# A six-deep weight ring for the last two jobs of the attention output projection, and one set of row buffers for w_o

## The chip, the core and the metric

The kernel runs on one core of a Trainium2 chip. The engines named below are TensorE (PE, with its weight loads shown as PEld), VectorE (DVE), ScalarE (ACT), GpSimd (POOL) and SyncE (SP, which issues most DMA transfers; ACT issues some). Each engine carries out its own instructions in the order in which they stand, and waits on semaphores for the others. The metric is the device time of one execution in microseconds (us), the median of several runs.

## The reference

One layer of a decoder block on a sequence of 2048 positions with 1024 channels:

```python
proj = h @ w_in[l]
...
y_rnn = (hr * jax.nn.silu(z_rnn.astype(jnp.float32))).astype(dt) @ w_out_rnn[l]
...
o = dilated_attention_mixture(qh, kh, vh).reshape(B, S, D_ATTN)
y_attn = (o * jax.nn.silu(z_attn.astype(jnp.float32))).astype(dt) @ w_out_attn[l]
...
merged = jax.nn.sigmoid(g_r + bg_r) * y_rnn + jax.nn.sigmoid(g_a + bg_a) * y_attn
x = x + gate[:, None, :] * (merged @ w_o[l])
return rms_norm(x, g_final)
```

The part that matters here is the product with `w_out_attn` (the second half of its columns), the merging behind it, and the product with `w_o`.

## The kernel before

Every fp32 product is made of three matmuls (`mm3`): each factor is split into a high part, rounded by ACT (`hi_act`), and a low part, the difference, made by DVE or POOL (`lo_dve`, `lo_pool`); high x high, high x low and low x high are added in PSUM.

The projections with `w_out_rnn` and `w_out_attn` are the generator `steps(jobs)`. A job is one of the two weight matrices with 512 positions; there are eight, the last four for attention. A job has 8 output tiles of 128 x 512, a tile 8 steps (one block of 128 input channels each), a step 3 matmuls. The weights of a tile come in two halves of 4 steps. Halves are numbered through all jobs by `x`; the last two jobs are tiles 48 to 63 (`TAIL0` is 48), steps 0 to 127 and halves 96 to 127. The first six jobs are worked off in between the attention heads; the last two run alone, one after the other, with the preparation of the output projection beside them.

Halves up to `RAW` = 97 come already split from DRAM (`wD`, 512 KB each). Later ones come raw (`wR`, 256 KB) and are split in place: `load_w(x)` loads into the second plane of the tile, `split_w(x)` writes the high part into the first plane and the low part over the raw values. The tiles of the ring are S0 to S3. `load_w(x + 3)` stands behind the first step of half x, `split_w(x + 1)` ahead of it; the low part is POOL's for every fourth half and DVE's else. The buffer that `load_w` writes was last read by half x - 1, so SP waits for PE there.

In the same steps: `load_g` loads two tiles (gaT and mrT, into the ring fg or into s1 and s2) for the eviction of a tile, `evict` multiplies the PSUM tile with one and adds the other (two DVE instructions), `store` writes the sum to meT; `load_y` and `split_y` load and split the 8 tiles of attention output for the next job (yh, yl; POOL for even, DVE for odd ones), around the boundary between the two jobs at step 64.

The output projection uses one level of Strassen's scheme. Its right factors (B11, B21, B22, T1 to T4, each high and low) are made of w_o in four builds, k = 0 to 3. A build takes two rows of w_o of 128 x 1024 (`load_rows(k)`, 512 KB each), multiplies each with the gate on POOL (`gate_rows`), combines their quarters on DVE (`combine`), and splits seven results (`high` on ACT; the low parts of B22, T3 and T1 on POOL, the others on DVE). The last two are those of T4 and T1. The rows stand in st1 and st2 for even k, in st3 and st4 for odd k; st0 holds the gate. `build_rows(s, k)` puts the pieces behind steps s to s + 16 of the last two jobs, with s = 10, 34, 74 and 98; the rows are loaded ahead of step 0 and behind steps 16, 44 and 75, by SP for k = 0 and by ACT else.

Behind the builds come the left factors of the first pair of rows of the output: `load_left(0)` loads two blocks of meT into st1 and st2 behind step 104, `left_events` sums and splits them into st3, st4, st0 and S0 to S3. Then the product phase begins: eight calls of `output_pair`, each with seven products of 12 matmuls into X, Z, W, V, X, Y and V. At its start a pool is opened, x rows and g_final are loaded by SP (`load_rows_x`), and then the A tiles of the second pair by `load_left(1)`, which is fired by `fire_p`.

All this stands under a manual schedule: the engines' queues are in the order in which the code calls the instructions. In each step of the last two jobs the generator's own instructions come first, then what `on(n, ...)` put behind that step.

Of the kernel before, what the change touches and what calls it, by code (L numbers as in the profile page):

```python
# [10 lines left out]
F32 = mybir.dt.float32  # L11
# [9 lines left out]
P = 128  # L21
S = 2048
# [67 lines left out]
def decoder_block(ctx, tc, x, c, positions, g_norm, w_mod, b_mod, w_in, b_gate, conv_w, conv_b,  # L90
# [1567 lines left out]
    def steps(jobs):  # L1658

        tiles = [(j, m) for j in range(len(jobs)) for m in range(KT)]  # L1660
        Y, G = {}, {}

        def load_w(x):

            if x < 2 * len(tiles):
                assert x == n_w[0]
                j, m = tiles[x // 2]
                if x <= RAW:
                    load_wd(jobs[j][0], m, x % 2)
                    return  # L1670

                n_w[0] += 1
                W[x] = t = T(pS, [P, 2, KH, P], F32R, f"S{x % 4}")
                nc.sync.dma_start(t[:, 1].bitcast(F32), wR[m, x % 2])

        def split_w(x):
            if RAW < x < 2 * len(tiles):
                raw = W[x][:, 1].bitcast(F32)
                hi_act(W[x][:, 0], raw)
                (lo_pool if x % 4 == 0 else lo_dve)(W[x][:, 1], raw, W[x][:, 0])  # L1680

        def load_y(j, k):
            if j < len(jobs):
                w, ys, n = jobs[j]
                if ys is oT and (n, k) == (2, KT - 1):

                    Y0[False, n, k] = last_head[0].zt[:, 0].rearrange("p r j -> p (r j)")
                    return
                if ys is oT and n == 2 and k >= KH:

                    t = T(ap_, [P, KQW], F32, "kraw", bufs=4)
                    nc.sync.dma_start(t[:, :CH], ys[k * P : (k + 1) * P, n * CH : (n + 1) * CH])
                    Y0[False, n, k] = t[:, :CH]
                    return
                assert ys is yaT or (n // 2, k, n % 2) in stored
                load_yd(ys, n, k)

        def split_y(j, k):
            if j < len(jobs):
                Y[j, k] = yh, yl = [T(fl, [P, CH], F32R, tag, bufs=NY) for tag in ("yh", "yl")]  # L1700
                w, ys, n = jobs[j]
                t = Y0.pop((ys is yaT, n, k))
                hi_act(yh[:], t[:])
                (lo_dve if k % 2 else lo_pool)(yl[:], t[:], yh[:])

        def load_g(t):
            j, m = tiles[t]
            w, ys, n = jobs[j]
            at_ = slice(m * P, (m + 1) * P), slice(n * CH, (n + 1) * CH)
            G[t] = []  # L1710
            for src in (grT,) if ys is yaT else (gaT, mrT):
                if t >= TAIL0 and (t - TAIL0) % 3 == 2 and t < TAIL0 + 13:
                    g = T(fp, [P, CH], F32, ("s1", "s2")[len(G[t])])
                else:
                    g = T(fl, [P, CH], F32, "fg", bufs=4)
                nc.sync.dma_start(g[:], src[at_])
                G[t].append(g)

        def evict(t, ps):
            g = G[t]  # L1720
            nc.vector.tensor_tensor(g[0][:], ps[:], g[0][:], ALU.mult)
            if len(g) > 1:
                nc.vector.tensor_tensor(g[0][:], g[0][:], g[1][:], ALU.add)

        def store(t):
            j, m = tiles[t]
            w, ys, n = jobs[j]
            nc.sync.dma_start((mrT if ys is yaT else meT)[m * P : (m + 1) * P, n * CH : (n + 1) * CH], G.pop(t)[0][:])

        g_loads = {(0, 0): [0], (14, 0): [14], (15, 0): [15]}  # L1730
        for x in range(13):
            g_loads[x, 3] = [x + 1]
        for k in range(KT):
            split_y(0, k)
        yield
        last = None
        for t, (j, m) in enumerate(tiles):
            ps = T(pj, [P, CH], F32, "pj")
            for k in range(KT):
                if k % KH == 0:  # L1740
                    split_w(2 * t + k // KH + 1)
                if k % KH == 1:

                    load_w(2 * t + k // KH + 3)
                if k == 1 and t:
                    evict(t - 1, last)
                if t < TAIL0:
                    if k == 3:
                        load_g(t)
                    if k == 7 and t:  # L1750
                        store(t - 1)
                else:
                    if k == 4:
                        store(t - 1)
                    for x in g_loads.pop((t - TAIL0, k), ()):
                        load_g(TAIL0 + x)
                wt = W[2 * t + k // KH]
                yh, yl = Y[j, k]
                mm3(ps[:], wt[:, 0, k % KH, :], wt[:, 1, k % KH, :], yh[:], yl[:], first=k == 0, last=k == KT - 1)
                if k % KH == KH - 1:  # L1760
                    W.pop(2 * t + k // KH)


                x = m * KT + k - KT * (KT - 1)
                j1 = j + 1
                if m == 0:
                    x, j1 = x + KT * KT, j

                if j1 == NB + 2:

                    if -14 <= x < KT - 14:
                        load_y(j1, x + 14)
                elif j1 and x in LOAD_Y:
                    load_y(j1, LOAD_Y[x])
                if j1 and x in SPLIT_Y:
                    split_y(j1, SPLIT_Y[x])
                yield
            last = ps
        evict(len(tiles) - 1, last)
        store(len(tiles) - 1)  # L1780
# [72 lines left out]
    v = {}  # L1853
    tt = nc.vector.tensor_tensor

    def load_rows(k):
        for i in range(2):
            v[k, i] = t = stage(1 + i + 2 * (k % 2), [P, D])
            (nc.scalar if k else nc.sync).dma_start(t[:], w_o[0, (k + i * KH) * P : (k + i * KH + 1) * P, :])

    def gate_rows(k, i):
        nc.gpsimd.tensor_tensor(v[k, i][:], v[k, i][:], v["gate"][:], ALU.mult)
# [26 lines left out]
    A, ops = {}, {}  # L1889
    NP = 2 * NB  # L1890

    def load_left(p):
        for half in range(2):
            shape = [P, KH, 2 * P]
            A[p, half] = t = T(up[0], shape, F32, f"A{half}", bufs=2) if p else stage(1 + half, shape)
            (nc.sync if p else nc.scalar).dma_start(t[:], meT[half * KH * P : (half + 1) * KH * P, p * 2 * P : (p + 1) * 2 * P]
# [164 lines left out]
    with tc.manual_schedule():  # L2061
        v["gate"] = stage(0, [P, D])
        nc.sync.dma_start(v["gate"][:], gateD[0:1, :].broadcast_to([P, D]))
        load_rows(0)
        for k in range(KH):
            build_rows((10, 34, 74, 98)[k], k)
            if k:
                on((16, 44, 75)[k - 1], load_rows, k)
        on(LAST - 24, load_left, 0)
        early = {}  # L2070
        for p in range(NP):
            for d, fn, args in left_events(p):
                x = 7 * p + d - 4
                if p or d > 2:
                    on_p(max(x, 1), fn, *args)
                else:
                    on(LAST - 12 + 4 * (d + 1), fn, *args)
            if p:
                on_p(max(7 * p - 12, 0), load_left, p)
            if p > 1:  # L2080
# [6 lines left out]
        assert not pend  # L2087
        pools.close("fl", "pR")
        up.append(pools.open("up", side="right", bufs=1))
        v["gf"] = T(up[0], [P, D], F32, "gf")  # L2090
        load_rows_x(0)
        load_rows_x(1)
        nc.sync.dma_start(v["gf"][:], g_final.unsqueeze(0).broadcast_to([P, D]))
        fire_p()
        for p in range(NP):
            output_pair(p)
        assert not after
# [30 lines left out]
```

## Time and profile before

| what | value |
| --- | --- |
| median of 3 runs | 2246.54 us (2245.64 to 2247.35) |
| the profiled execution | 2248.86 us |
| its span, first to last instruction | 2247.1 us, 34124 instructions |
| mean granted TensorE clock | 0.990 |
| the last two jobs, half 96 to the first product of the output projection | 1963.11 to 2083.84 us of the span |
| product phase | 2083.84 to the end |

In the views, a time is in us from the span's start. A row of the timeline has start, duration, engine, line, operation, output <- inputs, and in brackets the idle time ahead of it and what ended it. A row of the view of waits has who waited for whom, total us, number, longest. A row of the groups has busy us, mean ns of one, then idle us ahead of them with what ended it. L150 is the matmul in `mm`, L158 `hi_act`, L164 `lo_pool`, L167 `lo_dve`; L1674 is `load_w`, L1716 `load_g`, L1721 and L1723 the eviction, L1862 `gate_rows`. SPq and ACTq are issues of transfers. A row of the DMA view has the number of issues, KB each and median us from issue to landing.

### The profile page before, as it was taken

How to read it: one execution, taken by the hardware profiler on the slowest of the kernel's cores; microseconds unless marked ns; L12 is line 12 of the kernel's file. 1: busy time of each engine (PE TensorE's matmuls, PEld its weight loads, DVE VectorE, ACT ScalarE, POOL GpSimd, SP SyncE). 2: the span in 40 equal slices, each digit the busy share in tenths (PEclk: the TensorE clock that was granted, in tenths of full speed). 3: DMA queues.
4: the chain of work that ended last, by engine and by line, in shares of the span. 5: the costliest groups of instructions: out<-in, count | busy, mean ns of one | idle time of the engine just before them, and what ended most of it. 6: DMA issues, size and time to landing. Idle time of an engine off the chain costs nothing. (4 is left out here: it accounts for less than half of the span.)

```text
span 2247.1 us, 34124 instructions
## 1 busy us (share of the span) xinstructions
PE 2179.4 (97%) x11326; PEld 1837.1 (82%) x11326; DVE 1437.4 (64%) x2475; ACT 1283.2 (57%) x2554; POOL 1072.3 (48%) x791
## 2 busy tenths in 40 slices
PE   8999999999999999999999999999999998978998
PEld 5998888888778988888788877888888887856786
DVE  5839887878455715445445352566667787678787
ACT  6638678767533627556547202676778877533333
POOL 2457677667556322222223112555556555445443
PEclk9999999999999999999999999999999999999999
DMA  8367887887998378898889989988988887877543
GB/s 285 117 213 261 280 302 265 299 279 259 327 285 281 107 234 277 274 298 287 284 299 300 355 294 293 282 270 248 275 257 262 248 255 220 262 253 237 178 163 113
DMA packets 412133, 577.34 MB, mean 257 GB/s; under 512 B 72406, under 2 KB 270258, under 8 KB 410932
## 3 DMA queue, kind: packets, MB, share of 16 engines
q1 hardware_dynamic: 369748, 446.75, 63.5%
q10 hardware_dynamic: 42016, 128.36, 14.9%
q8 instruction: 90, 1.47, 0.3%
q14 instruction: 87, 0.71, 0.1%
q0 software_dynamic: 192, 0.05, 0.0%
HBM read 356.92 MB, written 218.11 MB: 256 GB/s over the span
## 5 line engine op out<-in xcount | busy, mean ns | idle before, releaser
L150 PE MATMUL pj<-yh,S 128*128 128x512 f32 x1024 | 372.9, 410 | 24.0 <-ACT S L158 7.0
L164 POOL TENSOR_TENSOR S<-R,S 128x512 fp32r<-128x512 f32 x168 | 256.1, 1533 | 172.8 <-ACT S L158 66.7
L150 PE MATMUL X<-T,S 128*128 128x512 f32 x1344 | 327.4, 393 | 7.0 <-ACT u L384 3.6
L150 PE MATMUL V<-T,S 128*128 128x512 f32 x1344 | 324.4, 390 | 0.5 <-DVE t L454 0.3
L150 PEld LDWEIGHTS X<-T,S 128*128 128x128 f32 x1344 | 253.1, 189 | 62.8 <-ACT u L384 5.1
L150 PEld LDWEIGHTS V<-T,S 128*128 128x128 f32 x1344 | 252.0, 188 | 54.5 <-DVE t L454 0.7
L150 PEld LDWEIGHTS pj<-yh,S 128*128 128x128 f32 x1024 | 194.7, 191 | 68.5 <-ACT S L158 9.0
L150 PE MATMUL pj<-yl,S 128*128 128x512 f32 x512 | 205.1, 401 | 8.7 <-POOL yl L164 5.6
L164 POOL TENSOR_TENSOR S<-s,S 128x512 fp32r<-128x512 f32 x92 | 139.7, 1518 | 112.4 <-ACT S L158 72.0
L1421 ACT ACTIVATE pp<-pp,st 128x256 f32<-128x256 f32 (+3 forms) x256 | 133.8, 524 | 93.4 <-DVE st L1420 92.2
L150 PE MATMUL Y<-T,S 128*128 128x512 f32 x672 | 163.2, 392 | 0.0
L150 PE MATMUL Z<-T,S 128*128 128x512 f32 x672 | 161.9, 390 | 0.0
L150 PE MATMUL W<-T,S 128*128 128x512 f32 x672 | 161.6, 389 | 0.0
L150 PEld LDWEIGHTS Y<-T,S 128*128 128x128 f32 x672 | 127.1, 190 | 26.5
L150 PEld LDWEIGHTS W<-T,S 128*128 128x128 f32 x672 | 126.0, 188 | 27.0 <-issue 0.9
L150 PEld LDWEIGHTS Z<-T,S 128*128 128x128 f32 x672 | 125.8, 188 | 26.0
L167 DVE TENSOR_TENSOR ptl<-pT,pth 128x384 fp32r<-128x384 f32 (+1 forms) x160 | 97.9, 629 | 75.1 <-ACT pth L158 72.8
L164 POOL TENSOR_TENSOR s<-R,s 128x512 fp32r<-128x512 f32 x32 | 45.5, 1421 | 207.3 <-ACT s L158 176.4
L912 DVE SCALAR_TENSOR_TENSOR xc<-xr,par,xc 128x512 f32<-128x512 f32 x96 | 98.4, 1025 | 48.4 <-ACT xc L906 46.2
L158 ACT ACTIVATE S<-R 128x512 fp32r<-128x512 f32 x168 | 101.6, 622 | 45.6 <-DMA R<-in_w_in_dram 20.0
L1485 ACT ACTIVATE pp<-pp,M 128x256 f32<-128x256 f32 (+3 forms) x256 | 118.0, 523 | 9.9 <-DVE M L1608 9.9
L150 PEld LDWEIGHTS pj<-yl,S 128*128 128x128 f32 x512 | 98.4, 192 | 28.2 <-POOL yl L164 8.3
(401 smaller groups left out, 4867.0 us busy)
## 6 DMA issues: line engine op xcount, KB each, us to landing
sD<-S ACTq DMA_DIRECT2D x196, 512.0 KB, 4.2
S<-sD SPq DMA_DIRECT2D x196, 512.0 KB, 5.2
S<-wD SPq DMA_DIRECT2D x98, 512.0 KB, 5.5
R<-in_w_in_dram SPq DMA_DIRECT2D x136, 256.0 KB, 4.2
wD<-s ACTq DMA_DIRECT2D x64, 256.0 KB, 5.3
T<-in_w_mod_dram SPq DMA_DIRECT2D x8, 1024.0 KB, 11.8
vN<-ev SPq DMA_DIRECT2D x64, 128.0 KB, 2.8
zaT<-ev SPq DMA_DIRECT2D x32, 256.0 KB, 4.6
```

Of the source, the lines that this page charges most:

```text
L150: nc.tensor.matmul(o, lhsT=l, rhs=r, start=st, stop=sp, **kw)
L158: nc.scalar.activation(o, i, AF.Copy)
L164: nc.gpsimd.tensor_tensor(o, i, h.bitcast(F32), ALU.subtract)
L167: return nc.vector.tensor_tensor(o, i, h.bitcast(F32), ALU.subtract).ins
L912: nc.vector.scalar_tensor_tensor(xc, xr[:, i : i + CH], cw(i), xc, ALU.mult, ALU.add)
L1421: nc.scalar.activation(pdst, pdst, AF.Exp, bias=m_, scale=-1.0, accum_out=l_)
L1485: nc.scalar.activation(pp, pp, AF.Copy, scale=w)
```

## The change

The raw halves use a ring of six tiles, S0 to S3, st3 and st4. In the last two jobs, raw loads are five halves ahead of use (behind the first step of half x, half x + 5; behind the first step of half 96, halves 99, 100 and 101) and splits three ahead (behind the second step of half x, half x + 3; 98 in half 96, 99 and 100 in half 97). The low part is POOL's for odd halves and DVE's for even ones. As st3 and st4 belong to the ring, all four builds use st1 and st2 for their rows; a row is loaded behind step s - 8 or s - 4 of its build, with s = 8, 32, 68 and 92. The two blocks of meT are loaded behind steps 107 and 110, and the first left operands' steps are 118, 121, 124 and 127 instead of 116, 120, 124 and 128. At the start of the product phase `fire_p`, and with it the load of the A tiles, stands ahead of the loads of the x rows and of g_final.

```diff
-                W[x] = t = T(pS, [P, 2, KH, P], F32R, f"S{x % 4}")
+                i = (x - 2 * TAIL0) % 6
+                W[x] = t = T(pS, [P, 2, KH, P], F32R, f"S{i}") if i < 4 else T(fp, [P, 2, KH, P], F32R, f"st{i - 1}")
                 nc.sync.dma_start(t[:, 1].bitcast(F32), wR[m, x % 2])
...
-                (lo_pool if x % 4 == 0 else lo_dve)(W[x][:, 1], raw, W[x][:, 0])
+                (lo_pool if x % 2 else lo_dve)(W[x][:, 1], raw, W[x][:, 0])
...
-                if k % KH == 0:
-                    split_w(2 * t + k // KH + 1)
+                x = 2 * t + k // KH
                 if k % KH == 1:
 
-                    load_w(2 * t + k // KH + 3)
+                    if x < 2 * TAIL0:
+                        load_w(x + 3)
+                    for x1 in range(x + 3 if x == 2 * TAIL0 else x + 5, x + 6) if x >= 2 * TAIL0 else ():
+                        load_w(x1)
+                if k % KH == 2 and x >= 2 * TAIL0:
+                    for x1 in (x + 2, x + 3) if x == 2 * TAIL0 + 1 else (x + 2,) if x == 2 * TAIL0 else (x + 3,):
+                        split_w(x1)
...
-    def load_rows(k):
-        for i in range(2):
-            v[k, i] = t = stage(1 + i + 2 * (k % 2), [P, D])
-            (nc.scalar if k else nc.sync).dma_start(t[:], w_o[0, (k + i * KH) * P : (k + i * KH + 1) * P, :])
+    def load_rows(k, i):
+        v[k, i] = t = stage(1 + i, [P, D])
+        (nc.scalar if k else nc.sync).dma_start(t[:], w_o[0, (k + i * KH) * P : (k + i * KH + 1) * P, :])
...
-    def load_left(p):
-        for half in range(2):
+    def load_left(p, halves=range(2)):
+        for half in halves:
...
-        load_rows(0)
-        for k in range(KH):
-            build_rows((10, 34, 74, 98)[k], k)
-            if k:
-                on((16, 44, 75)[k - 1], load_rows, k)
-        on(LAST - 24, load_left, 0)
-        early = {}
+        for k, x in enumerate((8, 32, 68, 92)):
+            build_rows(x, k)
+            for i in range(2):
+                on(max(x - 8 + 4 * i, 0), load_rows, k, i)
+        on(107, load_left, 0, (0,))
+        on(110, load_left, 0, (1,))
...
-                    on(LAST - 12 + 4 * (d + 1), fn, *args)
+                    on(LAST - 10 + 3 * (d + 1), fn, *args)
...
-        v["gf"] = T(up[0], [P, D], F32, "gf")
+        fire_p()
         load_rows_x(0)
         load_rows_x(1)
+        v["gf"] = T(up[0], [P, D], F32, "gf")
         nc.sync.dma_start(v["gf"][:], g_final.unsqueeze(0).broadcast_to([P, D]))
-        fire_p()
```

## The prediction

> **What bounds the kernel now.** I began with the page: TensorE is busy for 97% of the span, so the question is where it stands still or runs slowly. The view of busy time by stretches was cut at the places the change touches: the whole of the last two jobs, then that stretch cut at the starts of halves 105, 111 and 114, and the first products behind it. (A half is one half tile of weights, numbered as in the code; halves 96 to 127 belong to the last two jobs. Columns: stretch, length, busy time and count of PE, PEld, DVE, ACT, POOL, granted clock, DMA share, GB/s.) The last row, from the chain of waits, is a product at full pace.
>
> ```profile
> PE 2179.4 (97%) x11326; PEld 1837.1 (82%) x11326; DVE 1437.4 (64%) x2475; ACT 1283.2 (57%) x2554; POOL 1072.3 (48%) x791
> ...
> 1963.11:2083.84 120.73, 100.45 (x386) 73.92 (x384) 93.42 (x97) 41.67 (x72) 61.50 (x34) 0.94 0.75 240
> 1963.11:2001.78 38.67, 30.40 (x110) 21.48 (x108) 23.47 (x26) 10.02 (x17) 16.41 (x9) 0.91 0.74 252
> 2001.78:2023.36 21.58, 17.51 (x74) 13.20 (x72) 20.79 (x21) 8.41 (x14) 11.54 (x7) 1.00 0.87 260
> 2023.36:2038.73 15.37, 11.51 (x37) 6.96 (x36) 9.54 (x9) 6.23 (x11) 8.75 (x5) 0.89 0.91 282
> 2038.73:2083.84 45.11, 41.03 (x170) 32.28 (x168) 39.61 (x43) 17.02 (x31) 24.80 (x14) 0.96 0.65 207
> ...
> 2112.64 2.72 PE V L150 x12
> ```
>
> Twelve matmuls take 2.72 us, so the 32 halves need 32 x 2.72 = 87.0 us; they take 120.73. The 33.7 us over are 14.2, 5.3, 7.2 and 7.0 in the four stretches (9, 6, 3 and 14 halves). Next the waits in this window, and then the rows of PE, SP and ACT around the costliest one.
>
> ```profile
> ACT S L158 <- DMA S<-wR: 40.4, 12, 6.9
> ...
> PE pj L150 <- ACT S L158: 7.0, 4, 2.6
> PE pj L150 <- DVE S L167: 5.3, 5, 2.3
> PE pj L150 <- POOL S L164: 4.0, 4, 1.7
> ...
> 1976.19 1.06 PE L150 MATMUL pj<-yh,S 128*128 128x512 f32 x2
> ...
> 1981.62 0.64 PE L150 MATMUL pj<-yh,S 128*128 128x512 f32 x1 [2.63 <-ACT S L158]
> ...
> 1966.23 0.33 SPq L1716 DMA_DIRECT2D fg<-mrT  x1
> 1966.61 0.43 SPq L1674 DMA_DIRECT2D S<-wR  x1
> 1967.81 0.32 SPq L1716 DMA_DIRECT2D fg<-gaT  x1
> 1976.15 0.32 SPq L1716 DMA_DIRECT2D fg<-mrT  x1
> ...
> 1977.04 0.89 SPq L1674 DMA_DIRECT2D S<-wR  x2
> ...
> 1980.94 0.63 ACT L158 ACTIVATE S<-S 128x512 fp32r<-128x512 f32 x1 [6.87 <-DMA S<-wR]
> ```
>
> PE waits for weights that are split late, and they are split late because ACT waits for raw loads. These are late in their turn because SP stood from 1967.81 to 1976.15 at the mrT load: its buffer comes free with an eviction on VectorE that is queued behind the split of half 99, which waits for the load issued at 1966.61. It is a loop: one late load delays the issue of the next. After such a wait PE also runs at half pace (two matmuls in 1.06 us, where 2.72/12 = 0.23 us apart is usual), and the first stretch's granted clock is 0.91.
>
> The other limit is the pair VectorE and GpSimd, which turn the rows of w_o into Strassen factors ("builds" 0 to 3) beside the jobs:
>
> ```profile
> 1997.58 1.71 POOL L164 TENSOR_TENSOR S<-S 128x512 fp32r<-128x512 f32 x1
> 1999.25 5.65 POOL L1862 TENSOR_TENSOR st<-st,st 128x1024 f32<-128x1024 f32 x2
> ...
> 2000.47 2.18 DVE L1723 TENSOR_TENSOR fg<-fg,fg 128x512 f32<-128x512 f32 x1
> 2002.57 3.48 DVE L167 TENSOR_TENSOR S<-S 128x512 fp32r<-128x512 f32 x2
> ...
> L164 POOL TENSOR_TENSOR S<-S 128x512 fp32r<-128x512 f32 x7 | 10.3, 1477 | 24.2 <-ACT S L158 19.2 <-DMA S<-wR 5.0
> L167 DVE TENSOR_TENSOR S<-S 128x512 fp32r<-128x512 f32 x23 | 25.7, 1125 | 17.9 <-ACT S L158 17.9
> ...
> 2025.35 1.30 POOL L164 TENSOR_TENSOR S<-S 128x512 fp32r<-128x512 f32 x1 [5.00 <-DMA S<-wR]
> 2005.98 0.68 DVE L167 TENSOR_TENSOR B11l<-st,B11h 128x512 fp32r<-128x512 f32 x1
> ```
>
> While GpSimd multiplies two rows, VectorE subtractions of 0.68 us take 2.18 and 3.48 for two: they end when the GpSimd instruction ends. So the two engines share one resource for these operations.
>
> **The change, part by part.** Outside the last two jobs nothing moves. Number and size of loads, matmuls and splits stay, so there the cost is nothing; what alters is where they stand.
>
> (1) Loads five ahead. Loads 99, 100 and 101 now go out together right behind the mrT load of 1966.23, ahead of the one that stood until 1976.15, so 100 and 101 are issued some 9 us earlier. That takes away the wait of 2.63 us and the slow matmuls behind it; the wait for half 99 (its load goes out at the same place) I leave. Later loads get 4.75 instead of 2.75 halves, 12.9 instead of 7.5 us, of which landing takes 4.3 (row below). SP still waits at each for PE to leave the buffer, at the same place in its queue, and what is behind it (mrT, gaT, stores) sees nothing new.
>
> (2) Splits three ahead, every second one on GpSimd: GpSimd gets 15 of them instead of 7, VectorE 15 instead of 23. A weight now may be late by 2.5 halves, 6.8 us, before PE notices. In the changed order half 105's subtraction stands on GpSimd right behind the last one (T1l) of build 0, half 111's right behind that of build 1, 127's behind that of build 3. So there PE waits for the build.
>
> (3) One set of row buffers. A row load now waits on ACT's queue until the build before has read the buffer; the second row's until T1l is done. ACT's splits of later halves are queued behind it. Before, it was issued half a build ahead. Exposed are: build 1's row, build 3's row, and the half of meT that the first left operands need. Build 2's is not: its rows come while GpSimd does the yl of the job boundary.
>
> (4) First left operands and, behind the jobs, A ahead of xo and gf in SP's queue.
>
> ```profile
> 1982.88 2.82 POOL L1862 TENSOR_TENSOR st<-st,st 128x1024 f32<-128x1024 f32 x1
> ...
> 1995.89 1.73 POOL L164 TENSOR_TENSOR T1l<-st,T1h 128x512 fp32r<-128x512 f32 x1 [4.53 <-ACT T1h L158]
> ...
> 2016.94 1.74 POOL L164 TENSOR_TENSOR T1l<-st,T1h 128x512 fp32r<-128x512 f32 x1 [3.81 <-ACT T1h L158]
> ...
> 2040.20 2.85 POOL L1862 TENSOR_TENSOR st<-st,st 128x1024 f32<-128x1024 f32 x1
> ...
> 2053.59 1.73 POOL L164 TENSOR_TENSOR T1l<-st,T1h 128x512 fp32r<-128x512 f32 x1 [4.54 <-ACT T1h L158]
> ...
> 2025.18 1.66 ACT L158 ACTIVATE yh<-R 128x512 fp32r<-128x512 f32 x3
> ...
> S<-wR SPq DMA_DIRECT2D x29, 256.0 KB, 4.3
> st<-in_w_o_dram ACTq DMA_DIRECT2D x6, 512.0 KB, 7.5
> R<-oT SPq DMA_DIRECT2D x8, 256.0 KB, 5.1
> ...
> S<-wD SPq DMA_DIRECT2D x98, 512.0 KB, 5.5
> ...
> 2086.56 0.39 PE L150 MATMUL Z<-T2h,st 128*128 128x512 f32 x1
> ...
> 2101.09 0.73 PE L150 MATMUL X<-B11h,st 128*128 128x512 f32 x2 [0.32 <-DVE st L167]
> 2107.36 0.73 PE L150 MATMUL Z<-T2h,st 128*128 128x512 f32 x2 [0.48 <-POOL st L164]
> ```
>
> What a lone row load takes is not shown: rows were loaded in pairs, 7.5 us each. Bounds: 4.3 (256 KB) and 7.5 (the pair); I take 5.5, as other 512 KB loads, plus 0.6 for semaphore and issue. From the end of the second row's product to T1l's end build 2 took 2055.32 - 2043.05 = 12.3 us and build 1 2018.68 - 2004.90 = 13.8; I take 12.3 (12.8 for build 3), since fewer late splits sit between. The sum follows this chain:
>
> Half 105: build 0's second row goes out at about 1977, behind the same mrT wait, and lands at 1981.3 to 1984.5; before, its product ran from 1982.88 to 1985.70, held by a split ahead of it in the queue. So T1l still ends at 1997.6. The split of 105 follows (1.3 to 1.7), and the half starts two matmuls before it: 1998.7, against 2001.78: 3.1 us ahead.
>
> Half 111: 1997.6 + 6.1 (row) + 2.8 + 12.3 = 2018.8 for T1l, split 2020.3, start 2019.9 against 2023.36: 3.5 ahead.
>
> Half 114: GpSimd does yl0 (to 2021.6), the split of 113 (2022.9), yl2 (2024.2); then y6 can be loaded (5.1), split (0.6 + 1.3): 2031.2; 114 starts 1.4 later, 2032.6 against 2038.73: 6.1 ahead. This needs the yh of 2025.18 to come earlier; it stood behind splits waiting for raw loads.
>
> First Z: two row products (5.2) and 12.3: T1l of build 2 at 2048.7; row 6.1, product 2.8, build 12.8: 2070.4; half of meT 6.1; two sums on VectorE, ACT and GpSimd (2 x 0.68 + 0.63 + 1.4 = 3.4): 2079.9 against 2086.56, 6.7 ahead. PE alone would be there at 2032.6 + 38.1 + 2.7 = 2073.4, and so waits; a half-pace stretch like that of 1976 behind such a wait costs up to 1.7 us. That leaves 5.0. A ahead of xo saves 0.5 of the waits of 0.32 and 0.48; the xo loads have cover, as they are added last.
>
> Sum: 5.5 us. The profiled execution took 2248.86 (span 2247.1), so 2243.4 by its own time. The median of the runs, 2246.54, lies 2.3 lower: 2241.0.
>
> The eight subtractions moved to GpSimd hold the shared resource for 1.30 (row at 2025.35) instead of 0.68 us (row at 2005.98) each, 5.0 us more together. I count those on the chain above and hold the rest covered by the row loads' landing. [...]
>
> **Rivals.** (a) Exposed rows decide: slower. If lone row loads land in 7.5 us too and builds take 13.8: T1l of build 1 at 1997.6 + 8.1 + 2.8 + 13.8 = 2022.3, half 111 level; 114 at 2036.1; T1l of build 2 at 2054.1, of build 3 at 2078.8; meT half 8.1, 3.4: Z at 2090.3, 3.7 late, with the slow stretch 5.4: 2252. It decides from about 6.5 us a row on. For it: DMA shares of 0.74 to 0.91. Against it: single loads instead of pairs.
> (b) The shared resource decides: no cover, 5.0 us back: 2246.0. For it: VectorE and GpSimd are busy for 93.42 + 61.50 us of 120.73. Against it: waiting for each other is counted in that (a split takes 1477 and 1125 ns in the mean, 1.30 and 0.68 us alone), and GpSimd stood idle for 24.2 us ahead of its seven splits.
> (c) Rows land in 4.3 us and no half-pace stretch: three exposures of 1.2 us less and 1.7: 2241.0 - 5.3 = 2235.7. For it: GB/s of 207 in the last stretch.
>
> **How the numbers follow.** Forecast 0.44 (its own range 2237 to 2245), (a) 0.14, (b) 0.25, (c) 0.17. A measurement of this kernel tells about 0.2%, 4.5 us, from no change: faster is below 2242.0, slower above 2251.0. Forecast: 0.34 faster, 0.10 same. (b): 0.04, 0.19, 0.02 slower. (a): 0.02 same, 0.12 slower. (c): all faster. Faster 0.55, same 0.31, slower 0.14. The range runs from 2232 ((c) with half 99's wait gone too) to 2251.5, just short of (a).
>
> **What would show it.** No PE wait at the start of half 100; 40.4 us of ACT waits on wR nearly gone; PE waits at 105 and 111 for POOL; a POOL or ACT wait for a lone w_o row of about 5 us in builds 1 and 3; PE waiting for Z's operand. Wrong if T1l of build 1 ends after 2021, if SP still stands ahead of loads 100 and 101, or if PE still waits at every second half.

## The result and the profile after

| | median, us | range, us | runs | ratio to before |
| --- | --- | --- | --- | --- |
| before, on the same chip | 2246.02 | 2245.19 to 2247.74 | 8 | |
| after | 2251.72 | 2248.41 to 2255.43 | 8 | 1.0024, interval 1.0013 to 1.0035 |

The change made the kernel slower by 0.24%, 5.7 us; the prediction was 2241.0. On another chip the same kernel came out at 1.0028 (interval 1.0014 to 1.0042), so the loss is the kernel's. The profiled execution of after took 2251.41 us, its span 2249.6 (before: 2248.86 and 2247.1).

These are the stretches of after: the last two jobs, and these cut at the starts of halves 105, 111 and 114, with the columns of the prediction's first view.

```profile
1962.02:2087.85 125.83, 101.34 (x386) 77.67 (x384) 95.07 (x89) 41.22 (x71) 72.35 (x40) 0.89 0.73 230
1962.02:2001.99 39.97, 28.96 (x110) 21.69 (x108) 22.82 (x23) 11.71 (x20) 18.07 (x11) 0.91 0.70 221
2001.99:2025.51 23.52, 18.97 (x73) 14.91 (x72) 20.79 (x21) 9.96 (x17) 17.21 (x10) 0.85 0.83 256
2025.51:2041.18 15.67, 11.21 (x38) 7.62 (x36) 9.95 (x8) 4.13 (x7) 9.12 (x6) 0.81 0.88 298
2041.18:2087.85 46.67, 42.21 (x170) 33.45 (x168) 41.51 (x40) 15.42 (x27) 27.95 (x16) 0.92 0.65 201
```

The last two jobs took 125.83 us instead of 120.73. Each of the four stretches is longer, by 1.3, 1.9, 0.3 and 1.6. The product phase, from there to the end of the span, took 161.8 instead of 163.3 us, 1.5 less; part (4) of the change stands there (see before_fire below).

Next, PE's waits in the last two jobs of after (who waits for whom, total us, times, longest).

```profile
PE pj L150 <- DVE s L1722: 6.5, 2, 4.5
PE pj L150 <- DVE fg L1722: 5.9, 2, 5.4
PE pj L150 <- ACT yh L158: 5.3, 3, 2.9
PE pj L150 <- ACT T4h L158: 3.4, 1, 3.4
PE pj L150 <- POOL S L164: 1.0, 2, 0.6
PE pj L150 <- ACT S L158: 0.9, 1, 0.9
...
```

The change did what it says to the waits for weights: 7.0 + 5.3 + 4.0 = 16.3 us became 1.0 + 0.9 = 1.9. But a wait that before does not have took their place: L1722 is the eviction. The first matmul of an output tile waits until the tile two earlier has been read, since these tiles have two PSUM buffers. With the one named T4h, at whose end VectorE had just done an eviction (it ended at 2074.16, the matmul started at 2074.31), these are 6.5 + 5.9 + 3.4 = 15.8 us. The waits for the next job's left operands (yh and, in the rows left out, yl) went from 3.8 to 6.5. All waits of the view together rose from 20.1 to 24.2 us, and PE's busy time rose from 100.45 to 101.34: nearly the whole 5.1 us. So the lower granted clock (0.89 instead of 0.94) shows in at most the 0.9 us of busy time.

The rows behind the longest wait, in after: those of SP, then VectorE, and one or two each of POOL, ACT and PE.

```profile
1967.01 0.38 SPq L1675 DMA_DIRECT2D S<-wR  x1
1967.44 0.90 SPq L1675 DMA_DIRECT2D st<-wR  x2
1968.39 0.84 SPq L1717 DMA_DIRECT2D fg<-gaT  x1
1978.90 0.32 SPq L1717 DMA_DIRECT2D fg<-mrT  x1
...
1979.74 0.43 SPq L1864 DMA_DIRECT2D st<-in_w_o_dram  x1
1980.27 0.93 SPq L1675 DMA_DIRECT2D S<-wR  x2
```

```profile
1974.81 1.26 DVE L167 TENSOR_TENSOR st<-st 128x512 fp32r<-128x512 f32 x1 [5.15 <-ACT st L158]
1975.99 0.68 DVE L1722 TENSOR_TENSOR fg<-pj,fg 128x512 f32<-128x512 f32 x1
1976.70 2.17 DVE L1724 TENSOR_TENSOR fg<-fg,fg 128x512 f32<-128x512 f32 x1
1985.96 1.64 DVE L167 TENSOR_TENSOR S<-S 128x512 fp32r<-128x512 f32 x1 [7.08 <-ACT S L158]
1987.53 0.68 DVE L167 TENSOR_TENSOR B11l<-st,B11h 128x512 fp32r<-128x512 f32 x1
1988.13 0.68 DVE L1722 TENSOR_TENSOR fg<-pj,fg 128x512 f32<-128x512 f32 x1
```

```profile
1975.48 2.85 POOL L1867 TENSOR_TENSOR st<-st,st 128x1024 f32<-128x1024 f32 x1
1984.71 2.35 POOL L1867 TENSOR_TENSOR st<-st,st 128x1024 f32<-128x1024 f32 x1 [4.68 <-DMA st<-in_w_o_dram]
1985.30 0.63 ACT L158 ACTIVATE S<-S 128x512 fp32r<-128x512 f32 x1 [6.31 <-DMA S<-wR]
1988.95 0.77 PE L150 MATMUL pj<-yh,S 128*128 128x512 f32 x1 [5.38 <-DVE fg L1722]
```

Read them from the top. Halves 99, 100 and 101 are loaded together at 1967.01 to 1968.34, as the prediction had it. SP then stands at the mrT load of tile 49 until 1978.90: 10.5 us after the gaT load, where before it was 8.3. It is released 0.03 us behind the end of the eviction of tile 48 (1976.70 + 2.17). That eviction stands on VectorE behind the split of half 100 (1974.81), which had itself waited 5.15; and its addition took 2.17 us instead of 0.69 (before, at 1975.43), as GpSimd was multiplying a row (1975.48). Behind the mrT load on SP stand the second row of build 0 (1979.74; POOL waits 4.68 for it) and the raw weights of halves 102 and 103 (1980.27). Those of 102 are split at 1985.30, VectorE takes the low part at 1985.96 after 7.08 idle, and only then, behind a low part of the build, at 1988.13, it evicts the tile that PE waits for. PE was free at 1988.95 - 5.38 = 1983.57: half 102's own weights, complete at 1987.60, come 4.0 us late, and the eviction queued behind them adds the last 1.3.

The wait at half 110 has the same form, without any late load (ACT's rows of after, then VectorE's and PE's):

```profile
2016.76 0.63 ACT L158 ACTIVATE T4h<-st 128x512 fp32r<-128x512 f32 x1 [1.79 <-DVE st L1875]
2017.30 0.61 ACT L158 ACTIVATE S<-S 128x512 fp32r<-128x512 f32 x1
```

```profile
2017.94 0.69 DVE L167 TENSOR_TENSOR S<-S 128x512 fp32r<-128x512 f32 x1 [0.61 <-ACT S L158]
...
2019.15 0.69 DVE L167 TENSOR_TENSOR T4l<-st,T4h 128x512 fp32r<-128x512 f32 x1
2019.76 0.69 DVE L1722 TENSOR_TENSOR s<-pj,s 128x512 f32<-128x512 f32 x1
2020.59 0.77 PE L150 MATMUL pj<-yh,S 128*128 128x512 f32 x1 [4.54 <-DVE s L1722]
```

Three halves ahead, the split of half 110 stands behind build 1's T4 on ACT, so that it comes at 2017.30, after PE ran out at 2016.05. Behind it come two more pieces of the build and the eviction. The lead of three halves is given to the order in the queue, not to the time at which the split is made.

### The profile page after: what moved, and what is told of

It reads as the page before. It is cut to its first block, busy times and chain, and to the rows that moved or that the text cites. A ratio compares the mean times of both kernels' runs of the same rounds, so it can differ in the third digit from the quotient of the medians.

```text
span 2249.6 us, 34130 instructions
## 1 busy us (share of the span) xinstructions
PE 2176.6 (97%) x11326; PEld 1840.2 (82%) x11326; DVE 1441.9 (64%) x2467; ACT 1282.6 (57%) x2554; POOL 1084.3 (48%) x799
## 5 line engine op out<-in xcount | busy, mean ns | idle before, releaser
L150 PE MATMUL pj<-yh,S 128*128 128x512 f32 x944 | 347.1, 410 | 22.6 <-DVE s L1722 6.5
L150 PEld LDWEIGHTS pj<-yh,S 128*128 128x128 f32 x944 | 180.9, 192 | 60.2 <-ACT S L158 15.7
L150 PE MATMUL pj<-yl,S 128*128 128x512 f32 x472 | 188.8, 400 | 6.6 <-POOL yl L164 5.3
L150 PE MATMUL Y<-T,S 128*128 128x512 f32 x672 | 161.8, 390 | 0.0
L1420 DVE CUSTOM_DVE_ANT_0 pp<-sc,msk 128x256 f32<-128x256 f32 (+3 forms) x256 | 104.6, 449 | 23.9 <-PE sc L150 21.7
```

Source lines behind the costliest of these rows:

```text
L150: nc.tensor.matmul(o, lhsT=l, rhs=r, start=st, stop=sp, **kw)
L1420: nc.vector.tensor_tensor_reduce(pdst, s_ps, mask, 1.0, 3e38, ALU.add, ALU.min, m_)
```

## The experiments

Two rivals of the prediction give the first theories: A, exposed rows, and B, the resource that the prediction has VectorE and GpSimd share. From the trace came P: splits placed three ahead stand on VectorE in front of the evictions that two PSUM buffers wait for. L, which came out of the first experiments, puts the loss on one place: SP's standing at the mrT load of tile 49. All ratios are to before on the same chip. The table also has, from each profile, how long SP stood at that load (from the issue of the gaT load to that of the mrT load), when T1l of builds 0 and 3 ended behind the start of half 96, and the time from there to the first product (X).

| kernel | ratio (95% interval) | SP at mrT | T1l, build 0 | T1l, build 3 | half 96 to X |
| --- | --- | --- | --- | --- | --- |
| before | | 8.3 | 34.5 | 112.8 | 120.7 |
| after | 1.0024 (1.0013 to 1.0035) | 10.5 | 37.8 | 117.2 | 125.8 |
| after_again | 1.0028 (1.0014 to 1.0042) | 10.2 | 37.5 | 118.3 | 127.1 |
| after_psum4 | 0.9999 (0.9986 to 1.0012) | 10.1 | 38.5 | 118.3 | 124.0 |
| before_psum4 | 1.0002 (0.9991 to 1.0012) | 8.3 | 35.2 | 114.6 | 120.9 |
| after_split2 | 0.9980 (0.9968 to 0.9992) | 4.1 | 31.0 | 109.1 | 118.7 |
| after_split1 | 0.9979 (0.9968 to 0.9990) | 2.7 | 31.4 | 108.5 | 121.2 |
| after_gk5 | 0.9993 (0.9981 to 1.0005) | 4.1 | 31.7 | 112.6 | 120.2 |
| split2_gk5 | 0.9980 (0.9967 to 0.9993) | 1.7 | 29.5 | 110.3 | 119.9 |
| after_share | 0.9962 (0.9948 to 0.9976) | 8.1 | 33.5 | 110.3 | 117.2 |
| share_again | 0.9984 (0.9970 to 0.9997) | 8.4 | 35.0 | 112.3 | 119.1 |
| share_psum4 | 0.9986 (0.9975 to 0.9997) | 8.2 | 35.2 | 111.7 | 117.4 |
| share_split2 | 0.9980 (0.9969 to 0.9991) | 8.4 | 32.9 | 111.9 | 120.3 |
| share_gk5 | 0.9975 (0.9963 to 0.9986) | 4.4 | 30.9 | 109.6 | 117.4 |
| one_g | 0.9999 (0.9986 to 1.0011) | 4.3 | 34.1 | 113.8 | 121.5 |
| late100 | 0.9999 (0.9986 to 1.0012) | 4.4 | 34.2 | 113.6 | 121.3 |
| late100_psum4 | 0.9987 (0.9978 to 0.9997) | 4.1 | 32.3 | 112.4 | 118.1 |
| before_fire | 0.9990 (0.9980 to 1.0000) | 8.3 | 34.4 | 116.4 | 122.7 |
| before_odd | 0.9974 (0.9963 to 0.9985) | 5.6 | 30.0 | 106.5 | 114.3 |
| before_one_g | 0.9973 (0.9962 to 0.9984) | 5.4 | 28.9 | 109.6 | 115.9 |

A profile is one execution, and the start of half 96 alone wanders by several us from one to the next (1956 to 1970 here); the ratios decide, and the columns tell why.

### Four PSUM buffers for the last output tiles (after_psum4, before_psum4)

Odd tiles of the last two jobs use the buffers Z and W of the product phase beside the two of pj; in before_psum4 the same is done to the kernel before.

```diff
-            ps = T(pj, [P, CH], F32, "pj")
+            ps = T(px_, [P, CH], F32, "ZW"[t // 2 % 2]) if t >= TAIL0 and t % 2 else T(pj, [P, CH], F32, "pj")
```

> The changed kernel with four PSUM tiles instead of two for the output tiles of the last two jobs. Theory P (splits moved ahead stand in VectorE's queue in front of the eviction that frees the PSUM tile, so PE waits for evictions): the 15.8 us of PE waits at evictions (at halves 102, 104, 110, 120, 124) vanish, part comes back as waits for weights; PE reaches the job boundary 4 to 8 us earlier, the yh splits that wait for PE come earlier, and the kernel takes 2245 to 2248. Theory A (the row loads of the single buffer set decide): PE waits move but the builds' last subtractions end as before (1999.9, 2021.3, 2057.8, 2079.2 within 1 us), and so does the time, 2251 to 2253.

> The kernel before with the same four PSUM tiles. It has no PE wait for an eviction, so theory P expects no change: 2244 to 2248. Theory A expects the same; a gain of more than 2 us here would say that evictions held the kernel before as well.

0.9999 and 1.0002. No wait for an eviction is left in after_psum4, and the loss goes; in before the buffers change nothing, so they are no gain by themselves. With four buffers in both kernels, on one chip, the changed one is level with before: the loss needs the two buffers. The builds are as late as in after (38.5): this takes away a result of the late evictions, not their cause.

### Splits nearer to their use (after_split2, after_split1)

```diff
-                    for x1 in (x + 2, x + 3) if x == 2 * TAIL0 + 1 else (x + 2,) if x == 2 * TAIL0 else (x + 3,):
-                        split_w(x1)
+                    split_w(x + 2)
```

In after_split1 these lines are gone, and `split_w(x + 1)` stands ahead of the first step of each half, as in before.

> The changed kernel with splits two halves ahead instead of three, so that the split of a half stands behind, not in front of, the eviction on VectorE. Theory P: the wait at half 102 (5.4 us) shrinks below 2 us and those at 104 and 110 by half; waits for weights return for some of it; 2246 to 2250. Theory A: 2251 to 2254, since rows come as late as before and the weights have less lead.

> The changed kernel with splits one half ahead, as in the kernel before, and raw loads five ahead. Theory P: no PE wait at an eviction; waits for low parts from GpSimd at most odd halves; 0.998 to 1.001 of the kernel before, behind the version with splits two ahead. Theory A (row loads decide): 1.002 or more, as in the changed kernel, since the rows are loaded as there.

0.9980 and 0.9979, 0.44% under after. No PE wait for an eviction is left in either, with two PSUM buffers, and SP stands 4.1 and 2.7 us. PE waits for weights again (in after_split2 15.9 us in all, counting S and st), and the kernel is faster all the same.

### Later mrT and gaT loads (after_gk5, split2_gk5)

```diff
-            g_loads[x, 3] = [x + 1]
+            g_loads[x, 5] = [x + 1]
```

> The changed kernel with the loads of gaT and mrT for the next tile two steps later, behind the raw load of the same step, so that SP does not stand at mrT (until 1978.9) in front of the second row of build 0 and of the raw load 102. Theory P: row and load 102 go out near 1970 instead of 1980, build 0 ends 5 us or more earlier (T1l near 1995), the wait at half 102 goes: 2244 to 2248. Theory A: build 0 ends earlier, but builds 1 and 3 are as far behind as their row loads; 2249 to 2252.

> Splits two ahead and the gaT and mrT loads two steps later, both together. Theory P: the gains add in part, as both act on the first build: 0.996 to 0.998 of the kernel before, last subtraction of build 0 before 1990. If the loop at SP is broken by the later split alone, no gain over splits two ahead (0.998).

0.9993 and 0.9980. With the loads two steps later, the second row of build 0 and half 102 are ahead of them in SP's queue, and T1l of build 0 ends at 31.7 instead of 37.8. With splits two ahead the later loads add nothing: both edits take away the same thing.

### The share of GpSimd (after_share, share_again, before_odd)

after_share gives GpSimd the low part of every fourth half, as before had it; before_odd gives it that of every second half in the kernel before, which is the change's share alone.

```diff
-                (lo_pool if x % 2 else lo_dve)(W[x][:, 1], raw, W[x][:, 0])
+                (lo_pool if x % 4 == 0 else lo_dve)(W[x][:, 1], raw, W[x][:, 0])
```

> The changed kernel with the kernel before's sharing of the low parts (every fourth on GpSimd, the others on VectorE). Theory P: the waits at evictions stay, and grow where a split more stands on VectorE; 1.002 to 1.004 of the kernel before. Theory B (eight subtractions moved to GpSimd cost 5 us of the resource that GpSimd and VectorE share): that comes back, 0.999 to 1.001.

> After with the low parts on GpSimd only for every fourth half, once more, since its first six runs (0.9962) lie below every combination with it (0.9975 to 0.9986). If those six were drawn low: 0.997 to 0.999. If it is the best version: 0.9955 to 0.997.

> Before, with one thing of the change: the low parts of every second half, not every fourth, on GpSimd (15 instead of 7). Theory B: 1.001 to 1.004, with T1l of build 3 ending 2 to 6 us later behind the start of half 96 than before's 112.8. Theory P, with B no cost by itself: 0.999 to 1.001. VectorE, with eight subtractions fewer, as the bound of before: below 0.999.

after_share, at 0.9962, looked like the proof of theory B: undo the share, and build 3 ends 6.9 us earlier than in after. before_odd turned that over. The same share, eight subtractions more on GpSimd, given to the kernel before made it faster by 0.26%, and all four builds end sooner. Its rows on VectorE, then those of after_share, show what both edits have in common.

```profile
1979.36 0.69 DVE L1721 TENSOR_TENSOR fg<-pj,fg 128x512 f32<-128x512 f32 x1 [3.89 <-DMA fg<-gaT]
```

```profile
1969.75 0.69 DVE L167 TENSOR_TENSOR S<-S 128x512 fp32r<-128x512 f32 x1 [4.13 <-ACT S L158]
...
1971.08 1.22 DVE L1724 TENSOR_TENSOR fg<-fg,fg 128x512 f32<-128x512 f32 x1
```

In before the split in front of tile 48's eviction is that of half 99; before_odd sends it to GpSimd, and the eviction waits for its own operand alone. In after it is that of half 100, with its high part behind that of half 99 on ACT; after_share sends that one to GpSimd, and the one left in front (half 99) is ready earlier and runs before GpSimd's multiplication (1969.75, against 1971.71). So the parity seems to decide by what it puts in front of one eviction; this is read from the rows, no run isolates it. share_again, twelve runs instead of six, gave 0.9984: the two intervals overlap only between 0.9970 and 0.9976, so the first figure probably overstates the gain.

### Two edits together (share_psum4, share_split2, share_gk5)

> After, with both corrections: the low parts on GpSimd only for every fourth half, as before, and four PSUM buffers for the last two jobs' output tiles. Theory P (splits placed three ahead stand on VectorE in front of the evictions that two PSUM buffers wait for) and theory B (the moved subtractions lengthen the builds through the shared resource) are separate costs if the ratio to before is 0.992 to 0.995, with no PE wait on an eviction left of the 10.4 us. If the waits at evictions only took the place of waits for the builds, the ratio stays at 0.995 to 0.998 and T1l of build 3 ends no earlier than 110 us behind the start of half 96.

> After, with the low parts on GpSimd only for every fourth half and splits two ahead. Both theories, if their costs add: 0.992 to 0.995. If splitting two ahead already gave most of what sharing gives (fewer splits in front of the builds): 0.995 to 0.998, no better than either alone.

> After, with the low parts on GpSimd only for every fourth half, and the mrT and gaT loads issued two steps later in each tile. If SP's standing at the mrT load still costs: 0.993 to 0.995, and SP is not held for more than 4 us at any of these loads. If what it costs is hidden by the raw weights' five halves of lead: 0.995 to 0.998.

0.9986, 0.9980 and 0.9975: none of the three comes near the sum of its parts. These runs also test theory B with the other edits in place. share_split2 and after_split2 differ in the share alone, and both are at 0.9980. share_psum4 and share_gk5 lie 0.13 and 0.18% under after_psum4 and after_gk5, with intervals that overlap. So a small cost of the share is not excluded.

### One pair of loads, one split (after_again, one_g, late100)

one_g moves the mrT and gaT loads of tile 49 only, to behind the second row and half 102. late100 leaves all loads and makes the split of half 100, and no other, two ahead, so that it stands behind the eviction of tile 48.

```diff
-            g_loads[x, 3] = [x + 1]
+            g_loads[x, 3 if x else 5] = [x + 1]
...
-                    for x1 in (x + 2, x + 3) if x == 2 * TAIL0 + 1 else (x + 2,) if x == 2 * TAIL0 else (x + 3,):
+                    for x1 in (x + 2, x + 3) if x == 2 * TAIL0 + 2 else (x + 2,) if x < 2 * TAIL0 + 2 else (x + 3,):
```

> The changed kernel itself, beside the three below. The experiments so far stand against before on other chips than the one on which after was 0.24% slower. If the loss belongs to the kernel: 1.001 to 1.004. If it belongs to that chip: 0.999 to 1.001, and the gains of the single edits over after are then smaller than read so far.

> After, with one thing moved: the mrT and gaT loads of the second of the last sixteen tiles are issued two steps later, behind the second row of build 0 and the raw weights of half 102. Theory L (SP's standing at this one mrT load, 10.5 us, delays build 0 and the next raw weights, and the rest follows from that): at least 0.2% better than after_again, T1l of build 0 ends 30 to 33 us behind the start of half 96 instead of 37.8. Theory P (the evictions' waits, wherever they fall): the later waits at evictions (halves 104, 110, 124) stay, so no more than 0.1% better. Theory B (the moved subtractions): no change.

> After, with the split of half 100 alone two ahead, so that on VectorE it stands behind the eviction that the mrT load waits for, not in front of it; all other splits three ahead. Theory L: SP stands at this load for 4 to 6 us instead of 10.5, T1l of build 0 ends 30 to 33 us behind the start of half 96, and the ratio is at least 0.2% under after_again. Theory B, or P at the later tiles: within 0.1% of after_again.

1.0028, 0.9999 and 0.9999. Either edit alone ends 0.29% under after_again and brings the changed kernel level with before. The builds came 3.4 us sooner, not the 5 to 8 expected. In late100 SP and VectorE read so:

```profile
1971.51 0.77 SPq L1717 DMA_DIRECT2D fg<-gaT  x1
1975.88 0.32 SPq L1717 DMA_DIRECT2D fg<-mrT  x1
...
1977.45 0.43 SPq L1864 DMA_DIRECT2D st<-in_w_o_dram  x1
```

```profile
1974.44 0.69 DVE L1722 TENSOR_TENSOR fg<-pj,fg 128x512 f32<-128x512 f32 x1 [2.05 <-PE pj L150]
...
1977.89 1.24 DVE L167 TENSOR_TENSOR st<-st 128x512 fp32r<-128x512 f32 x1 [2.04 <-ACT st L158]
```

The eviction now starts when PE has finished the tile, the split of half 100 follows it, and SP stands 4.4 us. What the edit gives is as large as the loss of the change, within intervals of some 0.13% either way. Whether it also is that loss takes the same edit in the kernel before, further down.

### Are the evictions a second cost? (late100_psum4)

> late100 with four PSUM buffers for the last two jobs' output tiles, as in after_psum4. In late100 PE still waits 12.5 us for evictions (halves 102, 104, 110, 124). Theories L and P as two separate costs of about 0.29% each: 0.996 to 0.998. If PE's waits at evictions only stand in for waits on what comes next (late weights, the left operands of the next job, Z's operand): 0.999 to 1.001, and other PE waits grow by about as much as these go.

0.9987, between the two expectations; its interval overlaps that of late100 (0.9999). PE's waits in late100, then in late100_psum4 (W and Z are output tiles there):

```profile
PE pj L150 <- DVE s L1722: 7.7, 2, 4.6
...
PE pj L150 <- ACT T4h L158: 3.4, 1, 3.4
PE pj L150 <- DVE fg L1722: 1.4, 1, 1.4
```

```profile
PE W L150 <- ACT S L158: 2.9, 1, 2.9
PE Z L150 <- POOL S L164: 2.3, 2, 1.6
...
```

12.5 us of waits for evictions went (with the one named T4h), and waits for weights, 1.2 us before, came to some 11: the weights of the same half are late in front of the eviction, as at half 110 above. The last two jobs became 3.2 us shorter, the product phase 1.7 longer. So most of the waits for evictions only stood in for waits on late weights, as far as these two profiles show.

### The loop in the kernel before (before_one_g), and the A loads (before_fire)

before_one_g is one_g's one line in the kernel before; before_fire moves `fire_p` ahead of the loads of x and g_final there, and nothing else.

> Before, with the mrT and gaT loads of the second of the last sixteen tiles issued two steps later, the edit of one_g alone. If the loop of late loads at SP, as the prediction read it, is worth in before what the prediction put on it (3 us at half 105, with what follows): 0.996 to 0.9985, T1l of build 0 ends about 31 us behind the start of half 96 instead of 34.5. If SP's stand there costs before nothing, since the splits come late anyway: 0.999 to 1.001.

> The kernel before with the loads of the second pair's left operands ahead of the x rows and g_final alone. The prediction's term: the waits of 0.32 and 0.48 us at the second pair's first products vanish or nearly, 0.3 to 0.8 us, 0.9996 of the kernel before; more than 2 us would be unexplained.

0.9973 and 0.9990. The order of SP's queue in before_one_g:

```profile
1965.00 0.32 SPq L1674 DMA_DIRECT2D S<-wR  x1
1965.95 0.32 SPq L1716 DMA_DIRECT2D fg<-gaT  x1
1971.36 0.32 SPq L1716 DMA_DIRECT2D fg<-mrT  x1
```

The raw weights of half 100 go out at 1965.00, ahead of the mrT load, the wait of 2.63 us at half 100 and the slow matmuls behind it are gone (two take 0.62 us at 1975.06), and T1l of build 0 ends 5.6 us sooner. The loop that the prediction found was worth 6 us, and moving one pair of loads takes it. The A loads brought 0.1%, though the interval reaches 1.0000; the product phase of that profile is 161.8 us as in after.

The same edit, then, gives 0.27% in the kernel before and 0.29% in the changed one. With the edit in both, the changed kernel is still 0.26% slower (0.9999 against 0.9973, each measured against before on its own chip; some 0.17% either way). So the held mrT load is a cost of both kernels, of about the same size, and theory L does not explain why after is slower than before. These are the last two jobs of before_one_g, then of one_g:

```profile
1960.12:2076.05 115.93, 97.22 (x385) 72.69 (x384) 94.79 (x97) 40.04 (x69) 61.38 (x33) 0.96 0.80 250
1966.34:2087.86 121.52, 101.05 (x385) 77.90 (x384) 91.62 (x87) 41.12 (x70) 72.35 (x40) 0.90 0.74 235
```

one_g takes 5.6 us more. PE is busy for 3.8 us more of that, at a lower granted clock (0.90 against 0.96). Of its waits 11.0 us are for evictions (halves 104, 110 and 124), where before_one_g has none. after_split2, after_split1 and split2_gk5, whose splits stand nearer to their use, have no such waits and are at 0.9979 to 0.9980, level with before_one_g within the intervals. With after_psum4 and before_psum4, which are level with each other, this points to the splits' lead of three halves, by way of the evictions behind them, as what the change itself costs. How much of that is the evictions and how much the pieces of the builds behind the same splits, no run isolates.

## Why the prediction was wrong

It said 2241.0; the runs gave 2251.72. The chain it followed can be laid beside after's rows: T1l of builds 0 and 1 and the subtraction of the third left operand at the boundary on POOL, the loads and ACT's high parts of the same operands, and a row of the DMA view.

```profile
1998.58 1.28 POOL L164 TENSOR_TENSOR T1l<-st,T1h 128x512 fp32r<-128x512 f32 x1 [4.53 <-ACT T1h L158]
2019.98 1.28 POOL L164 TENSOR_TENSOR T1l<-st,T1h 128x512 fp32r<-128x512 f32 x1 [4.52 <-DMA st<-wR]
...
2026.31 1.74 POOL L164 TENSOR_TENSOR yl<-R,yh 128x512 fp32r<-128x512 f32 x1
```

```profile
2029.10 0.93 SPq L346 DMA_DIRECT2D R<-oT  x2
...
2036.85 1.16 ACT L158 ACTIVATE yh<-R 128x512 fp32r<-128x512 f32 x2 [2.09 <-DMA R<-oT]
```

```profile
st<-in_w_o_dram ACTq DMA_DIRECT2D x6, 512.0 KB, 5.4
```

- **The first step that failed, part (1): SP "sees nothing new" behind the loads, and the loop goes.** The loop stayed; it lost halves 100 and 101 and took in others. The prediction moved the splits ahead on VectorE and did not ask what is queued behind a split there: the eviction that releases the mrT load. Held 10.5 instead of 8.3 us, SP now delayed the second row of build 0 and halves 102 and 103. one_g (two loads) and late100 (one split) take this standing away and end 0.29% lower than after. So the gain that part (1) counted on did not come. That the kernel even lost is another matter, since before had the loop too and gains as much without it.
- **Its share in part (3).** The second row was put at "about 1977, behind the same mrT wait", with T1l at 1997.6 still. It went out at 1979.74 and T1l ended at 1999.86, 3.3 us later when both are counted from the start of half 96 (37.8 instead of 34.5).
- **The second step that failed, part (2): "a weight now may be late by 2.5 halves, 6.8 us, before PE notices".** In the view of waits it looks right: 16.3 us of waits for weights became 1.9, and there is none at half 100. But VectorE's queue carries evictions too, and with two PSUM buffers PE notices those: 15.8 us of new waits. Half 102's weights were 4.0 us late all the same, with the wait put down to the eviction behind them. With four buffers in both kernels the loss is gone (0.9999 and 1.0002), with splits one or two ahead the kernel is at 0.9979 and 0.9980, and with the loop gone but splits three ahead it stays 0.26% behind before_one_g. So the loss comes by way of this step. How it divides among evictions, late weights and pieces of the builds behind the splits stays open: in late100_psum4 most of the waits for evictions only turned into waits for late weights, at a ratio of 0.9987, not clear of late100's 0.9999.
- **The boundary between the jobs, half 114.** From T1l of build 1 to half 114 the prediction took 2032.6 - 2018.8 = 13.8 us; after took 2041.18 - 2021.26 = 19.9, before 20.1, and in all twenty profiles it lies between 18.8 and 21.5. The term was under-sized by 6.1: four subtractions on POOL at 1.73 to 1.75 instead of 1.3 to 1.5 (1.4), the load of the last operands 1.0 behind the last of them, its landing in 7.7 instead of 5.1 (2.6), and the end on PE (1.0). That was larger than the whole sum, so the forecast would have been missed with the loop gone as well; one_g and late100, without the loop, are at 0.9999.
- **The other intervals held.** T1l of build 0 to that of build 1 was to take 21.2 us and took 21.4; half 114 to T1l of build 2, 16.1 and 16.6 (the two row products in it were put at 5.2, where the prediction's own row at 1999.25 has 5.65); build 2 to 3, 21.7 and 21.4. Lone rows landed in 5.4 us, where 5.5 was taken, so rival (a), whose time is the one that came, is not its cause: POOL's one long wait for a row is that for the row held by SP. The 0.6 us for semaphore and issue beside the 5.5 was the author's estimate. The 5.4 is counted from the start of the issue; beside it, in after, the second row of build 1 went out 0.03 us behind T1l's end (1999.86 to 1999.89), and POOL began 0.13 us behind the landing of the row it waited 4.68 us for (1984.58 to 1984.71).
- **Rival (b).** No cost of 5.0 us was found: before_odd has GpSimd's larger share and is 0.26% faster than before, and share_split2 and after_split2 are equal. A smaller cost can hide under the changed order. The blocking itself is there: the addition at 1976.70 took 2.17 instead of 0.69 us and ended 0.5 us behind GpSimd's multiplication, which ended at 1978.33. The prediction's two rows end 0.5 to 0.6 us behind GpSimd's too, not with them, and the first of them is an eviction's addition, not a subtraction. Over the last two jobs it is the same: every VectorE instruction of more than 1 us, 27 in before and 36 in after, ended 0.55 us behind the end of a GpSimd instruction, and none of them reads PSUM; the first steps of the evictions, which do, took 0.68 or 0.69 us, all 16 in each. That the moved work would show in the sum did not follow.
- **The end.** PE was to wait for Z's operand at 2079.9. It reached Z at 2090.57 with no wait there. PE waits at 105 and 111 for POOL did not come either: 105 followed half 104's wait for an eviction, 111 that of 110. Of the prediction's own signs of being wrong one came: T1l of build 1 ended after 2021, at 2021.26.
- **Part (4)** was taken as 0.5 us and measured 1.5 in the profile, 0.1% in before_fire.

With the loop undone (late100) the changed kernel is level with before, while before with one pair of loads moved is at 0.9973. So no version with the ring of six, the loads five ahead and the single row set is shown to be better than that move alone. Of all versions none is shown to be the best: before_one_g, before_odd, share_gk5 and after_share (0.9962, then 0.9984) overlap. T1l of build 0 ends at 34 us in one_g and at 31.7 in after_gk5; in one_g the split of half 99 already comes 2.4 us later (12.7 instead of 10.3 us behind the start of half 96), and the pieces of the build follow in the same order in both.

## What to carry to other kernels

An instruction placed earlier on an in-order engine is placed in front of something: before moving a step ahead, list what stands between its old and its new place, and who waits for that, DMA queues and PSUM buffers included. When a loop of late loads is found, the cheap test is to change the order at the one instruction that closes it, here one pair of loads two steps later, before building a deeper ring. And an edit that takes a loss away does not name its cause when several do. The same edit has to be made in the kernel before as well: there GpSimd's larger share made the kernel faster, and there the moved loads gained as much as in the changed kernel, so neither is shown to be what the change lost.

## What was not expected of the hardware

Most long waits of PE ahead of a half were followed by a slow stretch, and most short ones were not. Below are two waits of nearly one length: in before_one_g, and in after_gk5 (the rows from the wait on).

```profile
1971.44 0.50 PE L150 MATMUL pj<-yh,S 128*128 128x512 f32 x1 [2.52 <-ACT S L158]
```

```profile
2018.16 0.47 PE L150 MATMUL pj<-yh,S 128*128 128x512 f32 x1 [2.54 <-DVE s L1722]
...
2018.74 1.05 PE L150 MATMUL pj<-yh,S 128*128 128x512 f32 x2
```

Behind 2.54 us two matmuls take 1.05 us, at half pace (three in 1.28 us from 2018.74 on; 0.62 for two at 2023.04, once the stretch is over), and the half took 4.4 us instead of 2.7; behind 2.52 it took 3.2. In after, halves 102, 110 and 124 began with waits of 5.38, 4.54 and 3.40 us and took 5.3, 4.9 and 5.3, at a mean granted clock of 0.50, 0.54 and 0.50. In late100 halves 104 and 110, behind 4.55 and 3.19 us, took 4.4 and 4.3. In before, halves 103 and 109, behind 1.00 and 1.40 us, took 3.1 and 3.2, both at 1.00. So in these halves the waits of 2.54 us and more cost 1.5 to 2.5 us beyond their length (4.27 - 2.72 to 5.26 - 2.72). The length of one wait is not the whole rule: behind 1.98 us half 99 of before took 4.9, at 0.65, and behind 1.99 us half 104 of after took 2.8, at 1.00.
